# Weight sums stored from another queue, the last product's loads moved up, and a scale on another engine, in an encoder layer in float32

## The chip, the core and the metric

The kernel runs on one core of one Trainium2 chip. The metric is device time in microseconds (us) of one execution; lower is better. The engines are TensorE (PE; its weight loads are shown as PEld), VectorE (DVE), ScalarE (ACT), GpSimd (POOL) and SyncE (SP). SyncE, ScalarE and GpSimd each have a queue from which they issue DMA transfers; a queue's instructions are issued in their order, and one that waits holds up those behind it on its engine.

## The reference

One layer of a hybrid encoder for 512 frames of width 1024, in float32. The part that the change touches is the channel mixing at the end:

```python
u, g = jnp.split(x @ w_ffn_in[layer], 2, axis=-1)
h = jax.nn.gelu(causal_dwconv(u, conv_w[layer], conv_b[layer])) * g
x = layer_norm(DEEPNORM_ALPHA * x + h @ w_ffn_out[layer], ln2_g[layer], ln2_b[layer])
```

`w_ffn_in` is 1024 x 5632, so h is 512 x 2816 and `w_ffn_out` 2816 x 1024. Ahead of it stand an input projection, two attention branches with their gates, an output projection and a first layer norm.

## The kernel before

**Precision.** Each float32 operand is split into a rounded part (`hi`, on ScalarE, L103) and the remainder (`lo`, on VectorE, L105). A product of two operands takes three matmuls: hi x hi (L817), hi x lo (L818) and lo x hi (L819). Weights come in by SyncE's queue: class `Stream` loads them up to three pieces ahead into three `raw` buffers (L85), then splits them into a ring of three pairs of tiles. A load waits until VectorE has split the earlier content of its `raw` buffer.

**The feed-forward loop.** The 2816 inner columns are 22 chunks of 128. For each, `ffn_in` (L727 to L729) makes u and g, `activate` applies convolution and GELU, and two chunks form one of 11 pairs.

**The last matrix product** is done by a scheme in which seven products of sums and differences of blocks replace eight products of blocks: the tokens are halved, the rows of `w_ffn_out` go in the two chunks of a pair, and its 1024 columns are halved. Three of the products run in the loop (`second_half`, into PSUM tiles m3, m4 and m1) with weights that `mix_weights` (L777 to L779) forms from a `raw` and a `rawb` tile. The other four need h of all pairs, which is kept in `eh` and `el`, and follow the loop, each over six units of two pairs (the last has one):

- v, into m5, and y, into m2, with weights loaded from `w_ffn_out`;
- x, added into m1, with a sum of three weight blocks;
- z, added into m3, with another sum of weight blocks.

The sums for x and z are formed in the loop by `keep_sums` (L787 to L793): `s7` for x, and for z at once its parts `sh` (ScalarE) and `sl` (VectorE). They are stored to DRAM tensors `s_sum` by L795, three stores of 256 KB a pair. After the loop x is loaded from there like a weight and split again. z is loaded by a second stream (L75) straight into its place, tiles `d`, of which there are six; for each unit there are two loads, the hi parts and the lo parts. The helper `tc.issue_after(st.load)` puts them in SyncE's queue behind the latest load of the first stream.

**The end.** `unit` does one unit of one of these products, for 256 tokens in two blocks of 128 (m1 to m5 thus have a tile for each block). `into` (L892, L894) adds a finished product to the residual `r`, one tile for each of four token blocks, and takes statistics of it (L896). `finish` normalizes a token block: aggregate (L650), variance plus epsilon (L652), its power of -1/2 on GpSimd (L653), then two VectorE passes (L657, L658) and a store from ScalarE's queue (L904). The second token block of z comes last. It is done in two halves of 256 columns, the first into m3, the second into a tile `m6_end` in a PSUM bank that is used anew. For the last token block `finish` splits the second pass: VectorE does 768 columns (L912), GpSimd the other 256 as a product with 1/sigma (L909) and a sum (L910), and three stores (L914) follow.

**Who sets the order.** The program is written in the order of the code, but a scheduler that simulates the engines puts each engine's instructions in a row; what the code fixes is the order of a queue's loads within a stream and the `issue_after` marks. So z's matmuls for the first token block stand among those of y, where the simulated times put them.

Of the kernel before, what the change touches and what calls it, by code (L numbers as in the profile page):

```python
# [13 lines left out]
AF = mybir.ActivationFunctionType  # L14
ALU = mybir.AluOpType
# [34 lines left out]
def r32(ap):  # L50
    return ap.bitcast(F32)
# [77 lines left out]
def tile_block(ctx: ExitStack, tc: tile.TileContext, xT, xN, w_qi, w_ki, w_t, w_v, w_br, w_o, w_fi, w_fo,  # L129
               bg, cw, rel, onehot, lnp, out):  # L130
    nc = tc.nc
# [24 lines left out]
    def pa(name):  # L156
        return psA.tile([128, 512], F32, tag="A", name=name)

    def pb(name):
        return psB.tile([128, 512], F32, tag="B", name=name)  # L160
# [21 lines left out]
    sums = [nc.dram_tensor(f"s_sum{u}", (3, min(2, NP - 2 * u), 128, 512), F32, kind="Internal").ap() for u in range(NU)]  # L182
# [14 lines left out]
    st = Stream(nc, rawp, ring, order, 3, 3, place, POOL_LO)  # L197
    zt = Stream(nc, rawp, ring, kept, 0, 0, place)
# [443 lines left out]
    def bcast(pool, row):  # L642
        t = pool.tile([128, D], F32, name=f"ln{row}")
        nc.gpsimd.dma_start(t, bass.AP(tensor=lnp.tensor, offset=lnp.offset + row * D, ap=[[0, 128], [1, D]]))
        return t

    def norm_stats(r, parts):

        mv = padded(dp, [128, 2], tag="mv", bufs=2, name="mv")
        nc.vector.bn_aggr(mv, parts)  # L650
        rstd = padded(dp, [128, 1], tag="rstd", bufs=2, name="rstd")
        nc.vector.tensor_scalar(rstd, mv[:, 1:2], EPS, None, op0=ALU.add)  # L652
        nc.gpsimd.tensor_tensor(rstd, rstd, mhalf, op=ALU.pow)  # L653
        return mv, rstd

    def norm_apply(dst, r, mv, rstd, g, b, c):
        nc.vector.scalar_tensor_tensor(dst[:, c], r[:, c], mv[:, 0:1], g[:, c], op0=ALU.subtract, op1=ALU.mult)  # L657
        nc.vector.scalar_tensor_tensor(dst[:, c], dst[:, c], rstd, b[:, c], op0=ALU.mult, op1=ALU.add)  # L658
# [124 lines left out]
    def keep_sums(i):  # L783
        def f(_):

            a, b = (t.rearrange("p (k n) -> p k n", k=2) for t in mixing[i])
            nc.vector.tensor_add(b[:, 0], b[:, 0], a[:, 0])  # L787
            whole_ = tp.tile([128, 512], F32, tag="s7", bufs=1, name=f"s7_{i}")
            nc.vector.tensor_add(whole_, a[:, 1], a[:, 0])
            hi = tp.tile([128, 512], F32R, tag="sh", bufs=1, name=f"sh{i}")  # L790
            lo = tp.tile([128, 512], F32R, tag="sl", bufs=1, name=f"sl{i}")
            nc.scalar.activation(hi, b[:, 0], AF.Copy)
            nc.vector.tensor_sub(lo, b[:, 0], r32(hi))  # L793
            for n, half in enumerate((r32(hi), r32(lo), whole_)):
                nc.gpsimd.dma_start(sums[i // 2][n, i % 2], half)  # L795
            return []
        return f

# [13 lines left out]
    def product(pss, h, w, start, stop, blocks=(0, 1), c=slice(0, 512)):  # L812
        (xh_, xl_), (wh, wl) = h, w
        for t in blocks:
            r = slice(t * 128, t * 128 + 128)
            o = pss[t][:, c]
            nc.tensor.matmul(o, xh_[:, r], wh[:, c], start=start, stop=False, skip_group_check=True)  # L817
            nc.tensor.matmul(o, xh_[:, r], wl[:, c], start=False, stop=False, skip_group_check=True)  # L818
            mm = nc.tensor.matmul(o, xl_[:, r], wh[:, c], start=False, stop=stop, skip_group_check=True)  # L819
        return mm.ins  # L820
# [17 lines left out]
    for f in range(FC):  # L838
        if f == 0:
            ups, gps_ = ps0[0], ps0[1]  # L840
        else:
# [5 lines left out]
            if f % 2 == 0:  # L847
                if f == 2:
                    m3, m1 = [[pb(f"{n}_ps{t}") for t in range(2)] for n in ("m3", "m1")]
# [11 lines left out]
    def unit(pss, row, key, u, w, blocks=(0, 1), c=slice(0, 512), start=True):  # L861
        for n in range(min(2, NP - 2 * u)):
            i = 2 * u + n
            part = [x[:, n * 512:n * 512 + 512] for x in w]
            mm = product(pss, (eh[i][:, row], el[i][:, row]), part, start and i == 0, i == NP - 1, blocks, c)
        return mm
# [22 lines left out]
    def into(j, c, ps, by, first=False, stats=None):  # L889
        r = x1[j][:, c]  # L890
        if first:
            nc.vector.scalar_tensor_tensor(r, r, ALPHA, ps, op0=ALU.mult, op1=ALU.add)  # L892
        else:
            nc.vector.scalar_tensor_tensor(r, ps, by, r, op0=ALU.mult, op1=ALU.add)  # L894
        if stats is not None:
            nc.vector.bn_stats(parts2[j][:, stats], r)  # L896

    def finish(j):
        r = x1[j]
        mv, rstd = norm_stats(r, parts2[j])  # L900
        if j < 3:
            for c in (slice(0, 512), slice(512, 1024)):
                norm_apply(r, r, mv, rstd, g2, b2, c)
                nc.scalar.dma_start(out[j * 128:(j + 1) * 128, c], r[:, c])  # L904
            return
        cs = (slice(0, SHARE // 2), slice(SHARE // 2, SHARE), slice(SHARE, 1024))
        for c in (slice(512, 1024), slice(0, 512)):
            nc.vector.scalar_tensor_tensor(r[:, c], r[:, c], mv[:, 0:1], g2[:, c], op0=ALU.subtract, op1=ALU.mult)
        nc.gpsimd.tensor_scalar(r[:, cs[2]], r[:, cs[2]], rstd, None, op0=ALU.mult)  # L909
        nc.gpsimd.tensor_add(r[:, cs[2]], r[:, cs[2]], b2[:, cs[2]])  # L910
        for c in cs[:2]:
            nc.vector.scalar_tensor_tensor(r[:, c], r[:, c], rstd, b2[:, c], op0=ALU.mult, op1=ALU.add)  # L912
        for c in cs:
            nc.scalar.dma_start(out[j * 128:(j + 1) * 128, c], r[:, c])  # L914
# [12 lines left out]
        unit(m5, 1, "v", u, w)  # L927
    g2, b2 = bcast(wp, 2), bcast(wp, 3)
    held = []
    for u in range(NU):  # L930
        unit(m1, 2, "x", u, st.get(f"x{u}"), start=False)
        if u == 0:
            for t in range(2):
                into(t, second_c, m5[t], 1.0, stats=1)
                into(t, first_c, m5[t], -1.0)
    m2 = [pa(f"m2_ps{t}") for t in range(2)]
    for u in range(NU):
        unit(m2, 0, "y", u, st.get(f"y{u}"))
        with tc.issue_after(st.load):
            held.append(zt.get(f"z{u}"))  # L940
        if u < 2:
            into(u, first_c, m1[u], 1.0, stats=0)
            finish(u)
    for u in range(NU):
        mm = unit(m3, 3, "z", u, held[u], (0,), start=False)
        if u == 0:
            for t in range(2):
                into(2 + t, first_c, m2[t], 1.0, stats=0)
                into(2 + t, second_c, m2[t], -1.0)
            into(3, slice(768, 1024), m3[1][:, 256:512], 1.0)  # L950
    into(2, second_c, m3[0], 1.0, stats=1)
    finish(2)
    lo_c, hi_c = slice(0, 256), slice(256, 512)
    end = [None, pb("m6_end")]
# [4 lines left out]
    with tc.issue_after(mm):  # L959
        for u in range(NU):  # L960
            unit(end, 3, "z", u, held[u], (1,), hi_c, start=True)
    into(3, slice(768, 1024), end[1][:, hi_c], 1.0, stats=2)
    finish(3)
    close(wc)
    close(ec)
# [68 lines left out]
```

## Time and profile before

| | |
|---|---|
| median of 3 runs | 773.91 us (773.15 to 774.04) |
| the profiled execution | 773.86 us |
| its span, first to last instruction | 771.7 us |
| mean granted TensorE clock | 0.995 |
| PE busy | 753.8 us |
| DVE busy | 563.6 us |
| ACT busy | 358.4 us |
| POOL busy | 136.3 us |
| DMA engines, mean | 139 GB/s |

All times inside the program are us from the span's start. A row of the timeline has start, duration, engine, line, operation, output <- inputs by the program's names (without buffer numbers: `m_ps` is any of m1 to m5, `d_z` the z weights), shape and count; in square brackets stands the idle time of the engine ahead of it, and what ended it. SPq and ACTq are the issuing of transfers by SyncE and ScalarE. Matmuls are pipelined: a row's duration is longer than the distance to the next one.

### The profile page before, as it was taken

Reading aid. Unit: us, or ns where it says so; the run is one execution under the profiler, and the core shown is the slowest. Engines: PE = TensorE matmul, PEld = TensorE weight load, DVE = VectorE, ACT = ScalarE, POOL = GpSimd, SP = SyncE. Lnnn points to the kernel's source line nnn. Section 1 sums busy time; section 2 is a strip of 40 time slices with the busy share of each in tenths; the row PEclk is TensorE's granted clock in tenths of the full one; section 3 lists DMA queues with packets and bytes.
Section 4 is the critical chain, followed back from the end, with each engine's and each line's share of the span. In section 5 each row is a group of like instructions: output and inputs, shape, how many; then the busy total and the mean of one; then the engine's idle time right before and its main releaser. Section 6 shows DMA issues by size and latency. Waiting matters only on the chain.

```text
span 771.7 us, 9924 instructions
## 1 busy us (share of the span) xinstructions
PE 753.8 (98%) x3597; PEld 630.3 (82%) x3597; DVE 563.6 (73%) x944; ACT 358.4 (46%) x568; POOL 136.3 (18%) x161
## 2 busy tenths in 40 slices
PE   8999999999999999999999999999999999999995
PEld 7788887788888888888888888888888888888874
DVE  5579999977666475548855778767877787777774
ACT  6445654666564756835311534434443344344410
POOL 2002534527814110000000000000000000000011
PEclk9999999999999999999999999999999999999998
DMA  7742332232323323116801453355335434535591
GB/s 247 233 148 82 109 110 69 69 110 82 110 96 112 107 77 123 61 65 215 319 1 42 164 178 124 136 178 175 123 139 177 169 127 141 178 135 190 193 379 59
DMA packets 36336, 107.08 MB, mean 139 GB/s; under 512 B 4536, under 2 KB 4936, under 8 KB 36288
## 3 DMA queue, kind: packets, MB, share of 16 engines
q1 hardware_dynamic: 29264, 87.08, 32.9%
q0 software_dynamic: 4448, 13.09, 4.9%
q10 hardware_dynamic: 2576, 6.29, 3.0%
q8 instruction: 28, 0.46, 0.2%
q14 instruction: 20, 0.16, 0.1%
HBM read 91.48 MB, written 12.87 MB: 135 GB/s over the span
## 4 chain that ended last, share of the span: by engine, by line
PE 75%; DMA 3%; DVE 2%; issue 0%; ACT 0%; POOL 0%; POOLq 0%; ACTq 0%
PE u_ps L728 5%; PE u_ps L729 5%; PE g_ps L729 5%; PE g_ps L728 5%; PE g_ps L727 5%; PE u_ps L727 5%; PE m_ps L818 4%; PE m_ps L819 4%; PE m_ps L817 4%; DMA d_z<-s_sum 3%; PE av_ps L426 2%; PE ga_ps L276 2%; PE ga_ps L277 2%; PE ga_ps L275 2%; PE o_ps L687 2%; PE o_ps L685 2%
## 5 line engine op out<-in xcount | busy, mean ns | idle before, releaser
L727 PE MATMUL u_ps<-x1h,whi_u 128*128 128x512 f32 (+1 forms) x192 | 71.5, 372 | 0.3 <-ACT x1h L710 0.3
L728 PE MATMUL u_ps<-x1l,whi_u 128*128 128x512 f32 (+1 forms) x192 | 71.4, 372 | 0.1
L729 PE MATMUL u_ps<-x1h,wlo_u 128*128 128x512 f32 (+1 forms) x192 | 71.3, 372 | 0.0
L727 PE MATMUL g_ps<-x1h,whi_g 128*128 128x512 f32 (+1 forms) x184 | 69.9, 380 | 0.0
L729 PE MATMUL g_ps<-x1h,wlo_g 128*128 128x512 f32 (+1 forms) x184 | 69.9, 380 | 0.0
L728 PE MATMUL g_ps<-x1l,whi_g 128*128 128x512 f32 (+1 forms) x184 | 69.9, 380 | 0.0
L727 PEld LDWEIGHTS u_ps<-x1h,whi_u 128*128 128x128 f32 x192 | 36.2, 188 | 6.7 <-ACT x1h L710 0.5
L728 PEld LDWEIGHTS u_ps<-x1l,whi_u 128*128 128x128 f32 x192 | 36.2, 188 | 6.5 <-DVE x1l L711 0.3
L729 PEld LDWEIGHTS u_ps<-x1h,wlo_u 128*128 128x128 f32 x192 | 36.2, 188 | 6.3
L729 PEld LDWEIGHTS g_ps<-x1h,wlo_g 128*128 128x128 f32 x184 | 34.6, 188 | 6.6
L728 PEld LDWEIGHTS g_ps<-x1l,whi_g 128*128 128x128 f32 x184 | 34.6, 188 | 6.5
L727 PEld LDWEIGHTS g_ps<-x1h,whi_g 128*128 128x128 f32 x184 | 34.6, 188 | 6.5
L415 DVE TENSOR_TENSOR ptl<-tr_ps,pth 128x512 fp32r<-128x512 f32 (+1 forms) x48 | 27.4, 594 | 13.6 <-ACT pth L414 13.5
L736 POOL MEMSET u<- 128x2 f32 x22 | 2.3, 108 | 183.9 <-DVE c L741 183.9
L105 DVE TENSOR_TENSOR wlo_u<-raw,whi_u 128x1024 fp32r<-128x1024 f32 x22 | 26.9, 1221 | 9.5 <-ACT whi_u L103 9.5
L103 ACT ACTIVATE whi_g<-raw 128x1024 fp32r<-128x1024 f32 x22 | 23.3, 1060 | 20.5 <-PE m_ps L819 13.7
L103 ACT ACTIVATE whi_pa<-raw 128x1024 fp32r<-128x1024 f32 x11 | 11.7, 1062 | 40.8 <-PE u_ps L728 32.3
L742 ACT ACTIVATE c<-c,cwt 128x512 f32<-128x512 f32 x22 | 15.8, 717 | 30.8 <-DVE c L741 30.8
L105 DVE TENSOR_TENSOR wlo_g<-raw,whi_g 128x1024 fp32r<-128x1024 f32 x22 | 26.8, 1218 | 3.9 <-ACT whi_g L103 3.9
L103 ACT ACTIVATE whi_u<-raw 128x1024 fp32r<-128x1024 f32 x22 | 23.3, 1059 | 13.4 <-PE u_ps L728 8.7
L467 POOL TENSOR_TENSOR beta<-beta,keep 128x1280 f32<-128x1280 f32 x8 | 20.5, 2567 | 48.7 <-DVE keep L466 43.2
L414 ACT ACTIVATE pth<-tr_ps 128x512 fp32r<-128x512 f32 (+1 forms) x48 | 23.5, 520 | 11.3 <-PE tr_ps L410 8.9
(562 smaller groups left out, 2224.1 us busy)
## 6 DMA issues: line engine op xcount, KB each, us to landing
raw<-in_w_fi_dram SPq DMA_DIRECT2D x44, 512.0 KB, 3.3
raw<-in_w_t_dram SPq DMA_DIRECT2D x32, 512.0 KB, 3.3
raw<-in_w_fo_dram SPq DMA_DIRECT2D x21, 512.0 KB, 3.4
rawb_p<-in_w_fo_dram SPq DMA_DIRECT2D x11, 512.0 KB, 4.0
d_z<-s_sum SPq DMA_DIRECT2D x10, 512.0 KB, 9.3
raw<-in_w_v_dram SPq DMA_DIRECT2D x8, 512.0 KB, 3.5
raw<-in_w_br_dram SPq DMA_DIRECT2D x8, 512.0 KB, 3.2
raw<-in_w_o_dram SPq DMA_DIRECT2D x8, 512.0 KB, 4.1
```

The source lines that it names most:

```text
L103: nc.scalar.activation(hi[:, :w], t[:, :w], AF.Copy)
L105: self.low = eng.tensor_sub(lo[:, :w], t[:, :w], r32(hi[:, :w])).ins
L414: nc.scalar.activation(th[:, :width], ps[:, :width], AF.Copy)
L415: lows = nc.vector.tensor_sub(tl[:, :width], ps[:, :width], r32(th[:, :width]))
L467: nc.gpsimd.tensor_mul(beta, beta, keep[:, 1:ATT + 1])
L727: nc.tensor.matmul(ps[:, c], wh[:, kc], x1h[:, k, c], start=(k == 0), stop=False)
L728: nc.tensor.matmul(ps[:, c], wh[:, kc], x1l[:, k, c], start=False, stop=False)
L729: nc.tensor.matmul(ps[:, c], wl[:, kc], x1h[:, k, c], start=False, stop=(k == KC - 1))
L742: nc.scalar.activation(c, c, AF.Gelu_apprx_tanh, bias=cwt[:, f, 3:4])
L817: nc.tensor.matmul(o, xh_[:, r], wh[:, c], start=start, stop=False, skip_group_check=True)
L818: nc.tensor.matmul(o, xh_[:, r], wl[:, c], start=False, stop=False, skip_group_check=True)
L819: mm = nc.tensor.matmul(o, xl_[:, r], wh[:, c], start=False, stop=stop, skip_group_check=True)
```

## The change

Three edits. The stores of the weight sums (L795) are issued by SyncE in place of GpSimd. The product with 1/sigma of 256 columns of the last token block (L909) runs on ScalarE, with the scale as a value for each partition, in place of GpSimd. And z's loads are placed earlier: behind the x units 0, 1, 3 and 5 and the y units 0 and 1, where before there was one behind each y unit. With it a sum of 256 columns of m3's second token block into the residual, which was among the z units, stands ahead of y.

```diff
-                nc.gpsimd.dma_start(sums[i // 2][n, i % 2], half)
+                nc.sync.dma_start(sums[i // 2][n, i % 2], half)
...
-        nc.gpsimd.tensor_scalar(r[:, cs[2]], r[:, cs[2]], rstd, None, op0=ALU.mult)
+        nc.scalar.activation(r[:, cs[2]], r[:, cs[2]], AF.Copy, scale=rstd)
...
+    def keep_z():
+        with tc.issue_after(st.load):
+            held.append(zt.get(f"z{len(held)}"))
+
     for u in range(NU):
         unit(m1, 2, "x", u, st.get(f"x{u}"), start=False)
+        if u in (0, 1, 3, 5):
+            keep_z()
         if u == 0:
...
+    into(3, slice(768, 1024), m3[1][:, 256:512], 1.0)
     m2 = [pa(f"m2_ps{t}") for t in range(2)]
     for u in range(NU):
         unit(m2, 0, "y", u, st.get(f"y{u}"))
-        with tc.issue_after(st.load):
-            held.append(zt.get(f"z{u}"))
+        if u in (0, 1):
+            keep_z()
...
-            into(3, slice(768, 1024), m3[1][:, 256:512], 1.0)
```

SyncE's queue after the loop, before: `s_sum0` to `s_sum5` are the units of the stored sums, `raw` tiles take those for x and the weights of y, `d_z0` to `d_z5` are z's units (x2 marks the two loads).

```order
L85 DMA raw_140_0_6384<-s_sum3 128x2x512
L85 DMA raw_141_0_6408<-s_sum4 128x2x512
L85 DMA raw_142_0_6426<-s_sum5 128x512
L85 DMA raw_143_0_6443<-in_w_fo_dram 128x2x512
L85 DMA raw_144_0_6461<-in_w_fo_dram 128x2x512
L85 DMA raw_145_0_6479<-in_w_fo_dram 128x2x512
L85 DMA raw_146_0_6493<-in_w_fo_dram 128x2x512
L75 DMA d_z0_6511<-s_sum0 128x2x512 x2
L85 DMA raw_147_0_6527<-in_w_fo_dram 128x2x512
L75 DMA d_z1_6545<-s_sum1 128x2x512 x2
L85 DMA raw_148_0_6561<-in_w_fo_dram 128x512
L75 DMA d_z2_6579<-s_sum2 128x2x512 x2
```

And the same queue now, from the load of x3 on:

```order
L85 DMA raw_140_0_6384<-s_sum3 128x2x512
L75 DMA d_z0_6402<-s_sum0 128x2x512 x2
L85 DMA raw_141_0_6411<-s_sum4 128x2x512
L75 DMA d_z1_6429<-s_sum1 128x2x512 x2
L85 DMA raw_142_0_6432<-s_sum5 128x512
L85 DMA raw_143_0_6449<-in_w_fo_dram 128x2x512
L75 DMA d_z2_6467<-s_sum2 128x2x512 x2
L85 DMA raw_144_0_6470<-in_w_fo_dram 128x2x512
L85 DMA raw_145_0_6488<-in_w_fo_dram 128x2x512
L75 DMA d_z3_6500<-s_sum3 128x2x512 x2
L85 DMA raw_146_0_6506<-in_w_fo_dram 128x2x512
L75 DMA d_z4_6524<-s_sum4 128x2x512 x2
```

Before, four of z's six units (z2 to z5) stand behind the last weight load; now z0 to z4 stand in front of the last two. On TensorE z0's products for the first token block follow the first two products of x2, and z1 to z5 are spread up to the y4 unit; the rest of y comes behind them.

VectorE's row from the last split of y (L105) to the sum of `m6_end`, before (`m2_ps0` and `m2_ps1` are y's tiles for the two token blocks, `m3_ps0` and `m3_ps1` z's; `r2` and `r3` are the residual of the third and the fourth token block):

```order
L105 TENSOR_TENSOR wlo_y5_6564<-raw_148_0_6561,whi_y5_6563 128x512
L894 SCALAR_TENSOR_TENSOR r2_3602<-m2_ps0_6491,r2_3602 128x512 x2
L894 SCALAR_TENSOR_TENSOR r3_3603<-m2_ps1_6492,r3_3603 128x512 x2
L896 BN_STATS parts2_2_6307<-r2_3602 128x6
L896 BN_STATS parts2_3_6308<-r3_3603 128x6
L894 SCALAR_TENSOR_TENSOR r3_3603<-m3_ps1_4218,r3_3603 128x256
L894 SCALAR_TENSOR_TENSOR r2_3602<-m3_ps0_4217,r2_3602 128x512
L896 BN_STATS parts2_2_6307<-r2_3602 128x6
L650 BN_AGGR mv_6663<-parts2_2_6307 128x2
L652 TENSOR_SCALAR rstd_6665<-mv_6663 128x1
L657 SCALAR_TENSOR_TENSOR r2_3602<-r2_3602,mv_6663,ln2_6380 128x512 x2
L658 SCALAR_TENSOR_TENSOR r2_3602<-r2_3602,rstd_6665,ln3_6382 128x512 x2
```

And now, from the second pair of sums on:

```order
L894 SCALAR_TENSOR_TENSOR r3_3603<-m2_ps1_6505,r3_3603 128x512 x2
L896 BN_STATS parts2_2_6307<-r2_3602 128x6
L894 SCALAR_TENSOR_TENSOR r2_3602<-m3_ps0_4217,r2_3602 128x512
L896 BN_STATS parts2_3_6308<-r3_3603 128x6
L896 BN_STATS parts2_2_6307<-r2_3602 128x6
L894 SCALAR_TENSOR_TENSOR r3_3603<-m3_ps1_4218,r3_3603 128x256
L650 BN_AGGR mv_6663<-parts2_2_6307 128x2
L896 BN_STATS parts2_3_6308<-r3_3603 128x6
L652 TENSOR_SCALAR rstd_6665<-mv_6663 128x1
L657 SCALAR_TENSOR_TENSOR r2_3602<-r2_3602,mv_6663,ln2_6380 128x512 x2
L658 SCALAR_TENSOR_TENSOR r2_3602<-r2_3602,rstd_6665,ln3_6382 128x512 x2
L894 SCALAR_TENSOR_TENSOR r3_3603<-m6_end_6674,r3_3603 128x256
```

The sum of the first 256 columns of the last block and its statistics, which before stood behind L658, now stand ahead of L652. The split of y5 is still ahead of the first row shown, and its matmuls now follow those of z for the first token block.

In the loop the three stores of a pair stand in SyncE's queue directly ahead of the next pair's load of `rawb` (in the second pair one load stands among them). On ScalarE the store of the last block's 256 columns stands between the two 384-column ones; before it stood behind both. No table load is added there.

## The prediction

> **What bounds the kernel now.** I read the page's busy line first, then the chain of work that ended last in order of time, then the end of the program in the timeline.
>
> ```profile
> PE 753.8 (98%) x3597; PEld 630.3 (82%) x3597; DVE 563.6 (73%) x944; ACT 358.4 (46%) x568; POOL 136.3 (18%) x161
> 600.00:620.00 20.00, 20.00 (x90) 16.58 (x89) 14.61 (x22) 8.04 (x12) 1.81 (x5) 1.00 0.49 171
> ```
>
> The matmul unit is busy for 98% of the span, and in the feed-forward loop (second row: busy time of PE, PEld, DVE, ACT, POOL in one stretch, then clock, DMA share, GB/s) for all of it. A change can win only where TensorE stands still: near the end. There the chain leaves PE for DMA:
>
> ```profile
> 729.96 0.45 PE m_ps L817 x2
> 732.37 7.86 DMA d_z<-s_sum
> 740.24 12.10 DMA d_z<-s_sum
> 752.38 0.50 PE m_ps L818
> 762.73 0.44 DVE r L894
> ```
>
> TensorE's own rows there (start, duration, tile, shape, idle time before):
>
> ```profile
> 714.84 0.39 PE L817 MATMUL m_ps<-d_x,eh 128*128 128x512 f32 x1
> 729.80 0.61 PE L817 MATMUL m_ps<-whi_y,eh 128*128 128x512 f32 x2
> 736.23 0.50 PE L817 MATMUL m_ps<-d_z,eh 128*128 128x512 f32 x1 [0.37 <-DMA d_z<-s_sum]
> 752.38 0.50 PE L818 MATMUL m_ps<-d_z,eh 128*128 128x512 f32 x1 [1.12 <-DMA d_z<-s_sum]
> 754.63 0.28 PE L817 MATMUL m_ps<-d_z,eh 128*128 128x256 f32 x1
> 762.42 0.28 PE L819 MATMUL m_end<-d_z,el 128*128 128x256 f32 x1
> ```
>
> Between the first x product and the first y product lie 66 matmuls: (729.80 - 714.84)/66 = 0.2267 us each, with no wait. To the first half-width product lie 165 of them, 37.40 us; the rows give 754.63 - 714.84 = 39.79. So TensorE loses **2.39 us** to waits for z weights, more than the 0.37 and 1.12 in the brackets, because a matmul that restarts is also slower to get going (0.50 for 0.39). The 66 half-width ones run at (762.42 - 754.63)/65 = 0.120 us.
>
> Why z comes late:
>
> ```profile
> 713.05 0.36 SPq L85 DMA_DIRECT2D raw<-s_sum  x1
> 734.74 7.87 SPq L75 DMA_DIRECT2D d_z<-s_sum  x8
> d_z<-s_sum SPq DMA_DIRECT2D x10, 512.0 KB, 9.3
> 713.00:733.00 20.00, 20.00 (x90) 16.55 (x89) 14.85 (x20) 7.95 (x8) 0.00 (x0) 1.00 0.58 188
> 733.00:752.00 19.00, 17.89 (x78) 14.17 (x76) 14.82 (x26) 2.75 (x3) 1.98 (x2) 1.00 1.04 384
> ```
>
> Eight of the twelve z loads are issued after 734.74 and take 9.3 us each: from 733 to 752 the DMA engines are full (share 1.04, 384 GB/s), while the 20 us before run at 0.58.
>
> **The change part by part.**
>
> *z loads moved up.* They now stand in SyncE's queue behind x3, x4, y0, y2, y3 and y4. What TensorE needs first is z0, which the new order puts behind the two first x2 products:
>
> ```profile
> 717.02 1.06 ACT L103 ACTIVATE whi_x<-raw 128x1024 fp32r<-128x1024 f32 x1 [0.26 <-DMA raw<-s_sum]
> 720.73 0.39 PE L818 MATMUL m_ps<-wlo_x,eh 128*128 128x512 f32 x1
> ```
>
> x3 is issued at 713.05 and taken up at 717.02. z0's two halves follow it; at 384 GB/s 512 KB take 1.37 us, so they land near 718.4 and 719.8. TensorE wants them at 720.73 and 720.96: about 1.1 us to spare, the smallest margin. From there each z unit adds 6 x 0.2267 = 1.36 us of TensorE work ahead of the x and y units behind it, which gives their loads and splits that much more time. Following the queue at 1.37 us per 512 KB from 713 on, z1 lands 1 us ahead of its use, and y0 to y5 and z2 to z5 are ready 2 us or more ahead; the last z is in SBUF by about 742 and used near 747.5. So the 2.39 us go, and TensorE's last product would start at 714.84 + 37.40 + 65 x 0.120 = 760.03 in place of 762.42. Bounds: 2.39 at best, nothing if each unit waits as long as now.
>
> *What is late next: VectorE.* Before, y ended long before z, so the third token block was finished while TensorE still multiplied:
>
> ```profile
> 747.92 0.39 PE L819 MATMUL m_ps<-whi_y,el 128*128 128x512 f32 x1
> 748.35 2.48 DVE L894 SCALAR_TENSOR_TENSOR r<-m_ps,r 128x512 f32<-128x512 f32 x4 [2.80 <-PE m_ps L819]
> 750.75 1.28 DVE L896 BATCH_NORM_STATS2 parts<-r 128x6 f32<-128x512 f32 x2
> 751.95 0.41 DVE L894 SCALAR_TENSOR_TENSOR r<-m_ps,r 128x256 f32<-128x256 f32 x1
> 756.53 0.15 DVE L652 TENSOR_SCALAR rstd<-mv 128x1 f32<-128x1 f32 x1
> 757.92 1.41 DVE L658 SCALAR_TENSOR_TENSOR r<-r,rstd,ln 128x512 f32<-128x512 f32 x2
> 759.25 0.41 DVE L894 SCALAR_TENSOR_TENSOR r<-m_ps,r 128x256 f32<-128x256 f32 x1
> 759.70 0.43 DVE L896 BATCH_NORM_STATS2 parts<-r 128x6 f32<-128x256 f32 x1
> 762.73 0.42 DVE L894 SCALAR_TENSOR_TENSOR r<-m_end,r 128x256 f32<-128x256 f32 x1 [2.61 <-PE m_end L819]
> ```
>
> In the new order z runs among x and y, and y's end moves behind it: ahead of the last product into m2's first block stand 161 full and 4 half matmuls, so it starts at 714.84 + 161 x 0.2267 + 0.48 = 751.82, and VectorE takes it up 0.43 later (748.35 - 747.92), at 752.25. From there it has, in its order: four L894 (750.75 - 748.35 = 2.40), four more full-width operations (half of that pace is 1.20 for two, so 2.40), a half-width L894, an aggregate and a half-width L896 (0.41 and 0.43 with little between: 0.9), and from L652 to the end of block 2 what it was, 759.25 - 756.53 = 2.72. Sum 8.42: VectorE comes to m_end at 760.67. TensorE would let it start at 760.03 + 0.31 (762.73 - 762.42) = 760.34. So VectorE is **0.33 us** late, and m_end's add moves from 762.73 to 760.67: **-2.06**. Bounds: -2.39 if VectorE isn't late; about -1.6 if its 0.9 and its pauses are 0.4 longer.
>
> *The 1/sigma product on ScalarE.*
>
> ```profile
> 764.22 0.92 POOL L653 TENSOR_TENSOR rstd<-rstd,mhalf 128x1 f32<-128x1 f32 x1 [6.47 <-DVE rstd L652]
> 765.25 0.96 POOL L909 TENSOR_SCALAR r<-r,rstd 128x256 f32<-128x256 f32 x1
> 765.51 1.17 DVE L912 SCALAR_TENSOR_TENSOR r<-r,rstd,ln 128x384 f32<-128x384 f32 x2
> 766.18 1.45 ACTq L914 DMA_DIRECT2D out_dram<-r  x3
> 766.29 0.97 POOL L910 TENSOR_TENSOR r<-r,ln 128x256 f32<-128x256 f32 x1
> 697.33 0.40 ACT L757 ACTIVATE gh<-sm 128x256 fp32r<-128x256 f32 x1
> ```
>
> GpSimd's 0.96 becomes ScalarE's 0.40 (an ACTIVATE of that shape), with a hand-over to each side of some 0.15: L910 ends near 766.83, not 767.26. But the order of the stores changes too: the 256-wide one now stands second, ahead of VectorE's second 384-wide one, so the third can issue only about 0.4 after 766.85, at 767.25; before, it issued at 766.18 + 1.45 - 0.34 = 767.29. I cost this edit at **nothing** (bounds -0.4 to +0.2); what hides it is VectorE's 1.17 and the queue of three stores. The Trainium skill speaks against it: "ScalarE: Activation LUTs", Rules for kernel authors, gives multiplications to VectorE and budgets 0.3 us for an ACTIVATE and 0.83 ns an element, an estimate of 0.51 us here; by it the sum would be 0.1 us worse. The trace's 0.40 stands.
>
> *Weight sums stored by SyncE.* It adds 33 issues of some 0.34 us to SyncE and takes 33 of 0.54 from GpSimd, which nobody waits for.
>
> ```profile
> 609.00 0.33 SPq L85 DMA_DIRECT2D rawb_p<-in_w_fo_dram  x1
> 609.27 0.54 POOL L795 DMA_DIRECT2D s_sum<-sl  x1
> 613.37 0.69 DVE L777 TENSOR_TENSOR rawb_p<-rawb_p 128x512 f32<-128x512 f32 x1 [3.26 <-DMA rawb_p<-in_w_fo_dram]
> 618.30 1.06 ACT L103 ACTIVATE whi_g<-raw 128x1024 fp32r<-128x1024 f32 x1 [0.38 <-PE g_ps L728]
> 618.55 0.69 DVE L746 TENSOR_TENSOR hp<-g_ps,c 128x512 f32<-128x512 f32 x1 [1.38 <-PE g_ps L729]
> ```
>
> The load of rawb already waited in this queue for the same operation (L793) that the store of sl waits for, so only the issue comes on top: rawb lands 0.4 to 1.1 us later and L777 with it. What covers it: VectorE idles 1.38 at L746 and ScalarE 0.38 at L103, both until TensorE frees a buffer. Cost **0**; if the cover were gone, 0.4 a pair, 10 pairs, 4 us.
>
> The sum goes against the profiled execution: 773.86 (span 771.7 and 2.2 around it; the median of the runs, 773.91, is the same) - 2.06 = **771.8**.
>
> **The rivals.**
>
> 1. *z lands late again, now among x.* The cover of z0 and z1 is 1 us. For it: the 9.3 us landings where the engines are full. Against: x3's 3.97. A wait of 0.6 to 1.5 leaves -1.5 to -0.6: 772.4 to 773.2, take 772.8. Chance 0.17.
>
> 2. *VectorE's tail is longer.* If it comes to m_end another 0.6 later, the gain is 1.45: 772.4. For it: 8.42 us of work in a window of 8.1. Against: each operation's row is known. Chance 0.08.
>
> 3. *Slower: stores hold back weight loads.* Place: SyncE's queue in the loop, at the three stores and the loads behind. It decides from the point where rawb is later by more than the 1.38 us for which VectorE then idles. sh's and sl's stores stand directly ahead of rawb: two issues (0.68 us) and twice 256 KB (0.68 each at 384 GB/s) are 2.0 us, 0.7 beyond VectorE's 1.38; if TensorE lost that in each of 10 pairs, +7 - 2.1: 778.8. The Trainium skill, "DMA: Bandwidth & Descriptors", Queues, rings and completion order, has the reason: descriptors of one issuing queue are taken in ring order, while different queues take turns, so a store on SyncE's queue stands ahead of the load. By that rule alone rawb is later; whether TensorE is, the idle times above decide, and they speak against it. Chance 0.06.
>
> 4. *More than forecast:* VectorE isn't late, and the third store issues 0.3 earlier: 771.2. Chance 0.07.
>
> **How the numbers follow.** The forecast has 0.62, its own range 771.3 to 772.3. About 0.2%, 1.55 us, is what a measurement of this kernel tells from no change, so faster means under 772.36. Faster: forecast 0.62 and rival 4, 0.07: 0.69. Same: rivals 1 and 2: 0.25. Slower: 0.06. The range of 771.0 to 773.2 takes in rivals 1, 2 and 4 and leaves out 3 and the ends.
>
> **What would show it.** Right: no row of PE waiting for d_z; z loads landing between 718 and 743; the DMA share from 713 to 733 near 0.9; no idle time before m_end's L894 on DVE; the span ending 9.0 us after m_end's add starts, as now (771.7 - 762.73); L909 on ACT near 0.4; PE full in the loop. Wrong: a bracket with DMA d_z on PE, PE idle in the loop beside SyncE's L795, or the time from m_end's add to the end changed by over 0.3.

## The result, and the profile after

The changed kernel takes 769.61 us (median of 5 runs, 769.0 to 769.86), the kernel before, run beside it, 774.04. The ratio is 0.9948, 95% interval 0.9933 to 0.9963; by this ratio it is faster by 4.0 us, 2.9 to 5.2 (4.4 by the medians). The prediction said 771.8, in a range of 771.0 to 773.2. Faster was right; the gain is about twice the forecast, and the time lies below the range.

The profiled execution took 769.0 us, with a span of 767.2. Its busy line, and the stretches whose rows the prediction showed (busy time of PE, PEld, DVE, ACT, POOL, then clock, DMA share, GB/s):

```profile
PE 752.5 (98%) x3597; PEld 629.9 (82%) x3597; DVE 564.0 (74%) x944; ACT 359.2 (47%) x569; POOL 117.5 (15%) x127
```
```profile
600.00:620.00 20.00, 20.00 (x90) 16.57 (x89) 14.79 (x20) 7.94 (x11) 0.20 (x2) 1.00 0.50 170
713.00:733.00 20.00, 20.00 (x90) 16.57 (x89) 13.83 (x19) 8.06 (x8) 0.00 (x0) 1.00 0.97 349
733.00:742.00 9.00, 9.00 (x41) 7.46 (x40) 9.00 (x16) 2.13 (x2) 1.98 (x2) 1.00 1.05 387
742.00:752.00 10.00, 10.00 (x47) 8.36 (x46) 3.13 (x5) 0.64 (x1) 0.00 (x0) 1.00 0.17 62
```

TensorE is full in every one of them, and the transfers that filled 733 to 752 now run from 713 to 742. TensorE's own rows after (first x product, first z product, last product) have no bracket:

```profile
714.14 0.62 PE L817 MATMUL m_ps<-d_x,eh 128*128 128x512 f32 x2
...
720.03 0.39 PE L817 MATMUL m_ps<-d_z,eh 128*128 128x512 f32 x1
...
759.35 0.28 PE L819 MATMUL m_end<-d_z,el 128*128 128x256 f32 x1
```

The last block on VectorE, ScalarE and GpSimd (the same timeline, by engine):

```profile
751.56 2.48 DVE L894 SCALAR_TENSOR_TENSOR r<-m_ps,r 128x512 f32<-128x512 f32 x4 [6.84 <-PE m_ps L819]
...
759.83 0.42 DVE L894 SCALAR_TENSOR_TENSOR r<-m_end,r 128x256 f32<-128x256 f32 x1
...
762.59 1.61 DVE L912 SCALAR_TENSOR_TENSOR r<-r,rstd,ln 128x384 f32<-128x384 f32 x2
```
```profile
762.26 0.51 ACT L909 ACTIVATE r<-r,rstd 128x256 f32<-128x256 f32 x1 [18.27 <-POOL rstd L653]
763.24 1.43 ACTq L914 DMA_DIRECT2D out_dram<-r  x3
```
```profile
762.85 0.94 POOL L910 TENSOR_TENSOR r<-r,ln 128x256 f32<-128x256 f32 x1 [0.62 <-ACT r L909]
```

The prediction left out what comes behind the last store: the program's closing instructions, which all stand at the program's last line (L1030 before, L1037 after). Of the view of that line, the two rows that matter; they give shortest, median and longest duration in ns, then the first and last start. Before:

```profile
L1030 POOLq DRAIN  x3: 46/93/4698, 766.2 to 771.5; - x3
L1030 SPq DRAIN  x3: 7/7/7, 769.5 to 771.2; - x3
```

After:

```profile
L1037 POOLq DRAIN  x3: 46/93/1965, 762.8 to 767.0; - x3
L1037 SPq DRAIN  x3: 7/7/7, 766.4 to 766.7; - x3
```

A DRAIN starts while the last work of its engine still runs, and ends behind it, as GpSimd's does here with L910. SyncE waits for every store to land and reaches its first DRAIN at 769.5 before, at 766.4 after. GpSimd's first DRAIN starts with L910 and lasts 4.698 us before, to 770.9, so **before, SyncE and everybody else waited 1.4 us for GpSimd**; after, it lasts 1.965, to 764.8, and SyncE is last. The difference between the two profiled executions, 773.86 - 769.0 = 4.86, by stretches of these rows and those of the prediction:

| stretch | before | after | change | forecast |
|---|---|---|---|---|
| start to the first x product | 714.84 | 714.14 | -0.70 | 0 |
| to TensorE's last product | 47.58 | 45.21 | -2.37 | -2.39 |
| to the sum of m_end (L894) | 0.31 | 0.48 | +0.17 | +0.33 |
| to SyncE's DRAIN, the last store landed | 6.77 | 6.57 | -0.20 | 0 |
| to the end of the span | 2.2 | 0.8 | **-1.4** | 0 |
| outside the span | 2.16 | 1.80 | -0.36 | 0 |

### The profile page after: what moved, and what is told of

Read it like the earlier page. It is cut to its first block, busy times and chain, and to the rows that moved or that the text cites. A ratio compares the mean times of both kernels' runs of the same rounds, so it can differ in the third digit from the quotient of the medians.

```text
span 767.2 us, 9904 instructions
## 1 busy us (share of the span) xinstructions
PE 752.5 (98%) x3597; PEld 629.9 (82%) x3597; DVE 564.0 (74%) x944; ACT 359.2 (47%) x569; POOL 117.5 (15%) x127
## 4 chain that ended last, share of the span: by engine, by line
PE 77%; DVE 4%; issue 0%; ACT 0%; DVEq 0%; ACTq 0%
PE u_ps L728 5%; PE u_ps L729 5%; PE g_ps L729 5%; PE g_ps L728 5%; PE g_ps L727 5%; PE u_ps L727 5%; PE m_ps L817 4%; PE m_ps L818 4%; PE m_ps L819 4%; PE av_ps L426 2%; PE ga_ps L276 2%; PE ga_ps L277 2%; PE ga_ps L275 2%; PE o_ps L687 2%; PE o_ps L685 2%; PE o_ps L686 2%
## 5 line engine op out<-in xcount | busy, mean ns | idle before, releaser
L105 DVE TENSOR_TENSOR wlo_u<-raw,whi_u 128x1024 fp32r<-128x1024 f32 x22 | 26.9, 1221 | 9.2 <-ACT whi_u L103 9.1
L105 DVE TENSOR_TENSOR wlo_g<-raw,whi_g 128x1024 fp32r<-128x1024 f32 x22 | 26.8, 1218 | 3.9 <-ACT whi_g L103 3.9
```

Of the source, the lines that this page charges most:

```text
L105: self.low = eng.tensor_sub(lo[:, :w], t[:, :w], r32(hi[:, :w])).ins
```

## The experiments

Theory 1: GpSimd's closing DRAIN lasts longer the more DMA transfers GpSimd issued in the program (44 before, 11 after), and the change shortened it by taking 33 away. Theory 2: it was long because GpSimd had both L909 and L910 just ahead of it. The first four kernels take the edits apart; they ran on one chip, beside 32 runs of the kernel before with a median of 773.44. Single runs of one kernel differ by nearly 4 us there (771.64 to 775.38), so the profiles decide more than the medians.

**Stores alone.** The kernel before with

```diff
-                nc.gpsimd.dma_start(sums[i // 2][n, i % 2], half)
+                nc.sync.dma_start(sums[i // 2][n, i % 2], half)
```

> The kernel before with the stores of the weight sums (L795) on SyncE's queue, and nothing else. Theory 1 (the last DRAIN on GpSimd takes some 0.085 us for each DMA transfer that GpSimd issued in the program: 3.7 us behind its last operation for 44 transfers in the kernel before, 1.0 for 11 in the kernel after): the DRAIN ends 1.0 us after L910, at 768.3, ahead of SyncE's last wait at 769.6, so the program ends 1.45 us earlier: 772.6. Theory 2 (the DRAIN was long because GpSimd had the product L909 as well as the sum L910 just ahead of it): the DRAIN stays at 3.7 us and the time at 774.0. Rival 3 of the prediction (stores hold back weight loads): slower than 774.0, with idle time of TensorE in the loop.

Measured: 771.78, ratio 0.9979 (0.9969 to 0.9989). Closing instructions, and the sum of m_end:

```profile
L1030 POOLq DRAIN  x3: 46/98/2004, 764.4 to 768.1; - x3
L1030 SPq DRAIN  x3: 7/7/7, 767.5 to 767.9; - x3
```
```profile
760.90 0.42 DVE L894 SCALAR_TENSOR_TENSOR r<-m_end,r 128x256 f32<-128x256 f32 x1 [2.61 <-PE m_end L819]
```

L909 is still on GpSimd, yet the DRAIN is down to 2.004. From m_end's sum to the end of the span (768.4) it takes 7.5 us, where the kernel before takes 771.7 - 762.73 = 8.97. Theory 2 falls. The stores do not slow the loop: TensorE is busy for 250.0 of the 250 us from 440 to 690, as before.

**z's loads alone.** The kernel before with the third edit, shown in part.

```diff
+        if u in (0, 1, 3, 5):
+            keep_z()
...
-        with tc.issue_after(st.load):
-            held.append(zt.get(f"z{u}"))
+        if u in (0, 1):
+            keep_z()
```

> The kernel before with z's loads (and the sum of 256 columns) moved up, and nothing else. Both theories: TensorE's last product 2.4 us earlier, VectorE's sum of m_end 2.2 us earlier, the rest of the end as before with a DRAIN of 3.7 us behind L910: 771.8, the forecast's own figure. If the early z loads are worth more than TensorE's waits for z: under 771.3.

Measured: 771.56, ratio 0.9984 (0.9973 to 0.9995), so 0.4 to 2.1 us faster. Its profile has no wait for z, 45.2 us from the first x product to the last product as in the kernel after, a DRAIN of 4.701, and 769.9 - 760.86 = 9.0 from m_end's sum to the end:

```profile
760.86 0.42 DVE L894 SCALAR_TENSOR_TENSOR r<-m_end,r 128x256 f32<-128x256 f32 x1
```

This is the kernel whose time the prediction added up, with the end as it was. Its time is near the forecast of 771.8, but the kernel before ran at 773.44 beside it: the gain is 1.2 by the ratio, and the forecast 2.06 lies just inside the interval.

**The scale alone.** The kernel before with

```diff
-        nc.gpsimd.tensor_scalar(r[:, cs[2]], r[:, cs[2]], rstd, None, op0=ALU.mult)
+        nc.scalar.activation(r[:, cs[2]], r[:, cs[2]], AF.Copy, scale=rstd)
```

> The kernel before with L909 on ScalarE, and nothing else. Theory 1: the third store no earlier, but L910 ends 3.96 us after m_end's sum starts (as in the kernel after) in place of 4.53, and the DRAIN of still 3.7 us with it, 0.57 us earlier: 773.5. Theory 2: the DRAIN shrinks to 1.0 us: 772.6. The prediction's cost for this edit was nothing: 774.0.

Measured: 772.8, ratio 0.9999 (0.999 to 1.0007): no difference that a measurement shows. In the profile the DRAIN is 4.663 us long, so, like that of z's loads alone, it does not depend on this edit; the end comes 770.7 - 762.28 = 8.4 us after m_end's sum in place of 8.97, because L910 and the DRAIN behind it start earlier:

```profile
L1030 POOLq DRAIN  x3: 46/98/4663, 765.3 to 770.5; - x3
```

**Everything but the stores.** The kernel after with L795 back on GpSimd, the first diff above the other way round.

> The kernel after with the stores of the weight sums back on GpSimd. Theory 1: the DRAIN is 3.7 us long behind L910 and ends 3.96 + 3.7 = 7.66 us after m_end's sum starts, and the program 0.75 later at 8.4, against 7.37 in the kernel after: 1.0 us slower than it, 770.6. Theory 2: as the kernel after, 769.6, DRAIN 1.0.

Measured: 770.87, ratio 0.9969 (0.9959 to 0.9979). The DRAIN is back at 4.658 us, and the end 767.8 - 759.32 = 8.5 us behind m_end's sum: 1.1 more than in the kernel after.

```profile
L1037 POOLq DRAIN  x3: 46/93/4658, 762.3 to 767.5; - x3
L1037 SPq DRAIN  x3: 7/7/7, 765.9 to 767.2; - x3
```

By their ratios the three edits alone gain 1.6, 1.2 and 0.1 us, 2.9 together where the change gains 4.0. The intervals are wide enough for the difference, so these runs do not tell whether the edits help one another.

The next kernels ask what of the transfers the DRAIN counts: their number, their bytes or their packets.

**66 tiny stores more.** The kernel after with

```diff
-            return []
+            return [nc.gpsimd.dma_start(tick[n:n + 1], whole_[0:1, 0:16]) for n in range(66 if i == NP - 1 else 0)][:0]
```

> The kernel after, and GpSimd also issues 66 one-row stores of 64 bytes to a scratch tensor that nobody reads, before the end begins (GpSimd is idle there). GpSimd then issues 77 transfers in place of 11. Theory 1a (the closing DRAIN grows with the number of GpSimd's transfers, 3.68 us behind L910 for 44 and 0.99 for 11, so 0.0815 each and 0.09 besides): DRAIN of 6.4 us behind L910, the end at 3.96 + 6.4 + 0.8 = 11.1 us after m_end's sum in place of 7.4, the time 3.7 us above the kernel after: 773.3. Theory 1b (it grows with the bytes that GpSimd moved): DRAIN 1.0, the time as the kernel after, 769.6. Theory 1c (with the DMA packets: 4448 before and 1808 after on GpSimd's queue, 1.02 ns each): in between, by how many packets the small stores make.

Measured: 814.4, ratio 1.0528 (1.0504 to 1.0553). The end is what theory 1a asked for, 810.3 - 799.18 = 11.1 us from m_end's sum (expected 11.1):

```profile
L1037 POOLq DRAIN  x3: 46/97/7361, 802.2 to 810.0; - x3
```
```profile
799.18 0.41 DVE L894 SCALAR_TENSOR_TENSOR r<-m_end,r 128x256 f32<-128x256 f32 x1
```

GpSimd's queue on the three pages (packets, MB, share), of before, of after and of this kernel:

```profile
q0 software_dynamic: 4448, 13.09, 4.9%
```
```profile
q0 software_dynamic: 1808, 4.44, 1.6%
```
```profile
q0 software_dynamic: 3920, 4.45, 2.3%
```

With the bytes of the kernel after and fewer packets than before, the DRAIN is longer than in either: it goes by the number of transfers. The time as a whole was missed by 41 us, and that is the experiment's own doing. SyncE issues no load between 729.47 and 758.33, and TensorE waits for z's weights:

```profile
764.26 0.80 PE L817 MATMUL m_ps<-d_z,eh 128*128 128x512 f32 x1 [18.82 <-DMA d_z<-s_sum]
```

The small stores read the last s7 and waited for one another's landing (41.1 us in 16 waits). The load of z1, issued at 758.33, waited for the landing of a small store: SyncE's waits for them before z's loads are 28.3 us, the longest 26.2. That z's tile lies where s7 lay would account for it, but this was not tried.

**One of three stores on GpSimd.** The kernel after with

```diff
-                nc.sync.dma_start(sums[i // 2][n, i % 2], half)
+                (nc.gpsimd if n == 2 else nc.sync).dma_start(sums[i // 2][n, i % 2], half)
```

> The kernel after with one of the three stores a pair (s7) on GpSimd: 22 transfers of GpSimd. Theory 1a: DRAIN of 0.09 + 22 x 0.0815 = 1.9 us behind L910; it ends 3.96 + 1.9 = 5.9 us after m_end's sum starts, ahead of SyncE's last wait at 6.6, so the time is that of the kernel after, 769.6.

Measured: 770.34, ratio 0.9957 (0.9944 to 0.9969), as the kernel after within the interval.

```profile
L1037 POOLq DRAIN  x3: 46/98/2867, 763.7 to 768.1; - x3
L1037 SPq DRAIN  x3: 7/7/7, 767.5 to 767.8; - x3
```

**No transfer on GpSimd.** The kernel after with `nc.gpsimd.dma_start` replaced by `nc.sync.dma_start` throughout.

> The kernel after with every DMA issue of GpSimd moved to SyncE (the 11 that are left are the small inputs and the window table at the start and four rows of layer-norm values). Theory 1a: DRAIN of 0.1 us behind L910; no gain from it, since SyncE's wait for the last store already ends last by 1.6 us; from m_end's sum to the end 7.4 as in the kernel after. The start may be some us longer, since SyncE's queue then waits for the window table with weight loads behind it: 769.6 to 775.

Measured: 771.07, ratio 0.9967 (0.9954 to 0.9979). The DRAIN hardly outlasts L910's 0.94, and the end is no earlier for it, 770.0 - 762.55 = 7.45 after m_end's sum; the profiled start (first x product at 716.81) was longer, as feared.

```profile
L1037 POOLq DRAIN  x3: 40/82/1051, 765.5 to 769.7; - x3
```

Eleven profiles together, the last kernel of this section left out (the DRAIN starts with L910, so L910's own duration is taken off):

| kernel | GpSimd's transfers | DRAIN less L910, us | m_end's sum to the end of the span, us |
|---|---|---|---|
| none on GpSimd | 0 | 0.11 | 7.45 |
| after; after again | 11 | 1.03; 1.02 | 7.37; 7.34 |
| stores alone; scale back | 11 | 1.03; 1.03 | 7.50; 7.48 |
| one of three | 22 | 1.93 | 7.58 |
| before; z alone | 44 | 3.73; 3.72 | 8.97; 9.04 |
| scale alone; all but stores | 44 | 3.72; 3.72 | 8.42; 8.48 |
| 66 tiny more | 77 | 6.42 | 11.12 |

The third column is 0.11 + 0.082 for each transfer, to 0.02 us. GpSimd's other instructions do not count: the kernel with no transfer still has 116 of them (POOL on its page; the kernel after has 127 with its 11 transfers), and its DRAIN is 0.11 behind L910.

**The scale back on GpSimd**, in the kernel after (the third diff the other way round), and **the kernel after once more** beside it:

> The kernel after with L909 back on GpSimd. Theory 1 (with 11 transfers of GpSimd the DRAIN is 1.0 us behind L910, wherever L909 runs): L910 ends 4.5 us after m_end's sum starts in place of 3.96, the DRAIN at 5.5, ahead of SyncE's last wait at 6.6; the third store issues 4.56 after it in place of 4.43. 0.1 us above the kernel after: 769.7. Theory 2 (the last operation on GpSimd makes the DRAIN long): DRAIN 3.7, 1.5 us above it.

> The kernel after, unchanged, beside the one above: 769.6. TensorE from the first x product to the last product 45.2 us in each profile (no wait for z), and the start, up to the last product of the first projection, anywhere between 23.2 and 24.4 us, as in the nine profiles so far; if the 0.8 us by which the kernel after started earlier belonged to the change, this profile would show 23.5 again.

Measured: 769.51 (ratio 0.9954, 0.9937 to 0.9972) and 769.11 (0.995, 0.9932 to 0.9969). With the stores off GpSimd the scale's place is worth 0.1 us in the profiles, 7.48 against 7.37 and 7.34, and nothing in the medians. The last product of the first projection (L241), by which the start is judged, in the profile of before, then of the stores alone, then of the kernel after once more:

```profile
24.31 0.34 PE L241 MATMUL qi_ps<-xh,wlo_qi 128*128 128x384 f32 x1
```
```profile
23.32 0.34 PE L241 MATMUL qi_ps<-xh,wlo_qi 128*128 128x384 f32 x1
```
```profile
23.93 0.34 PE L241 MATMUL qi_ps<-xh,wlo_qi 128*128 128x384 f32 x1
```

The second kernel starts as the first one does by its program, and is 1.0 us earlier; the third stands in between. What sets this start, and with it the 0.70 us in the table above, stays open. With up to 11 transfers on GpSimd the row stands at 22.91 to 23.93 in six profiles, with 22 or more at 24.31 to 24.52 in five; but everything but the stores, with 44, has 23.00, so that number alone does not decide it.

**A shorter end.** The kernel after with

```diff
-SHARE = 768
+SHARE = 896
...
-            nc.scalar.dma_start(out[j * 128:(j + 1) * 128, c], r[:, c])
+            (nc.sync if c is cs[2] else nc.scalar).dma_start(out[j * 128:(j + 1) * 128, c], r[:, c])
```

> The kernel after with the last block's share on ScalarE and GpSimd cut from 256 to 128 columns (VectorE's two operations are 448 wide in place of 384) and its store issued by SyncE. In the kernel after VectorE's second L912 takes 1.08 us beside GpSimd's L910 where the first takes 0.62, and the third store issues 4.43 us after m_end's sum starts. If L910 at half its width ends before the second L912 would start, that operation takes 0.66 and the last store issues about 4.1 after m_end's sum: 0.3 us faster than the kernel after, 769.3, hardly more than runs differ. If the second L912 is slow for another reason, it stays near 1.1: 769.6 or a little more.

Measured: 769.64, ratio 0.9955 (0.9941 to 0.9968): no better than the kernel after. L910 at half its width still takes 0.85 (0.94 before), the second L912 beside it 0.875 (the first 0.685), and VectorE's two operations together 1.48:

```profile
762.65 1.48 DVE L912 SCALAR_TENSOR_TENSOR r<-r,rstd,ln 128x448 f32<-128x448 f32 x2
```

The end comes 767.1 - 759.89 = 7.2 us after m_end's sum, 0.15 earlier; a measurement does not show that.

## Why the prediction was right or wrong

**z's loads: right, in mechanism and size.** TensorE loses no time to z, and 47.58 - 45.21 = 2.37 us go, against 2.39. z0's halves were to land at 718.4 and 719.8, for products from 720.73 on, all of it 0.70 later than in the profile after. The view of z's tiles there, loads and landings:

```profile
L75 SPq DMA_DIRECT2D d_z<-s_sum x12: 404/460/614, 712.7 to 735.4; - x12
...
DMA to landing us min/median/max: 5.0/6.3/8.8
```

The first load, issued at 712.7, lands at 717.7 at the earliest, and the first z product runs at 720.03 without a wait. The DMA share from 713 to 733 is 0.97 (I said near 0.9), and by 742 the transfers are nearly over (0.17 from there to 752). What I had not seen is that the 2.39 was itself one draw. TensorE in the profile of the stores alone, where z's loads stand as before:

```profile
713.89 0.62 PE L817 MATMUL m_ps<-d_x,eh 128*128 128x512 f32 x2
...
750.45 0.50 PE L818 MATMUL m_ps<-d_z,eh 128*128 128x512 f32 x1 [0.81 <-DMA d_z<-s_sum]
...
760.58 0.28 PE L819 MATMUL m_end<-d_z,el 128*128 128x256 f32 x1
```

The stretch takes 46.69 us here, and 46.94 in the profile of the scale alone; without waits for z it is 45.2 or 45.3 in every profile. So the edit saves TensorE 1.5 to 2.4 us, and 2.37 agrees so well with 2.39 because both start from the same profile of before.

**VectorE late at the end: right, a little too large.** y's sums start at 751.56, 37.42 after the first x product; forecast were 752.25 - 714.84 = 37.41. VectorE then needs 8.27 us to m_end's sum, not 8.42, and is 0.17 late, not 0.33. The mis-sized term is the 0.9 for the half-width sum, the aggregate and the half-width statistics, which took 0.78 (756.35 to 757.13). There is no idle time ahead of m_end's L894, as forecast.

**The scale on ScalarE: nothing, as forecast, though not as costed.** The ACTIVATE took 0.51, not the 0.40 of the row that I chose. That row has a constant for its scale, this one a value for each partition. The Trainium skill, "ScalarE: Activation LUTs", What ACT_TABLE_LOAD costs, gives 186 ns and 0.833 an element with constants, and 93 more for each operand of that kind: estimates of 0.40 and 0.49, and the trace agrees with both. In a kernel with 44 transfers of GpSimd the edit would shorten the end by 0.55 (8.42 to 8.48 in place of 8.97 to 9.04), because L910, and the DRAIN with it, starts 0.5 earlier behind m_end's sum; I had not seen this. Nor is the nothing reached as I reckoned. I had VectorE's L912 at 1.17 and the third store held up by the queue. In the kernel after the two L912 take 1.61 beside L910 and end at 764.20, and the third store, issued at 764.25, carries what the second of them wrote: 4.42 behind m_end's sum, where before it was 4.56. An earlier L910 and a later L912 nearly cancel.

**Stores on SyncE: the step that failed.** "It adds 33 issues of some 0.34 us to SyncE and takes 33 of 0.54 from GpSimd, which nobody waits for" and "Cost **0**". The first half held: TensorE is full in the loop, and the load of rawb takes no longer to land (page, median us to landing 3.7; 4.0 before), so rival 3 fell. Nine waits for it sum to 26.4 us, before to 25.9. Of the pair that the prediction quoted, SyncE's load, then the wait, 3.04 for 3.26, with the same cover behind it:

```profile
608.65 0.44 SPq L85 DMA_DIRECT2D rawb_p<-in_w_fo_dram  x1
...
612.43 0.69 DVE L777 TENSOR_TENSOR rawb_p<-rawb_p 128x512 f32<-128x512 f32 x1 [3.04 <-DMA rawb_p<-in_w_fo_dram]
...
617.85 0.69 DVE L746 TENSOR_TENSOR hp<-g_ps,c 128x512 f32<-128x512 f32 x1 [1.40 <-PE g_ps L729]
```

The Trainium skill's rule of ring order ("DMA: Bandwidth & Descriptors", Queues, rings and completion order), on which that rival stood, has no price that this trace shows: from the issue of the load to L777 it is 3.78 us behind the stores, and 4.37 before (609.00 to 613.37). The second half was wrong: at the very end everybody waits for GpSimd. 33 x 0.082 = 2.7 us of its DRAIN go, of which 1.4 had been on the path. The chain of before ended in this DRAIN, and I read past it:

```profile
766.25 1.01 POOLq L1030
```

The row shows 1.01 us, a slice of the instruction; the view of line 1030 shows all 4.698. My check "the span ending 9.0 us after m_end's add starts, as now" took this stretch for a constant without asking what fills it, and it is there that the trace after says no: 7.37.

**The rest of the gap.** With these 1.4 us the sum would have been 770.4, and the profiled execution took 769.0. The table gives 0.70 of the other 1.4 to the start, 0.20 to the landing of the stores and 0.14 to z and VectorE; 0.36 us lie outside the span. This part is nearly constant for one built kernel, and differs between kernels. In the mean it is 2.13 to 2.21 in the three without z's edit (before, stores alone, scale alone) and 1.77 to 1.84 in five with it (z alone, all but stores, after, scale back, a shorter end). But three more with z's edit, with 22, 77 and no transfers of GpSimd, have 2.14, 2.16 and 2.34. So z's edit may be worth these 0.36 too, yet does not decide them by itself, and what fills this part stays open; the prediction took it as unchanged. Rival 4, 771.2 with 0.07, was nearest in size, but of its mechanism, an earlier third store, only 0.14 us came (0.20 at its landing), and VectorE was late.

## What to carry to other kernels

Follow the chain of waits to the very last instruction, and view the closing line by engine: it costs time like any other, and here one engine's closing work was 1.4 us of a 4 us gain. An engine that nobody waits for during the program may be waited for at its end, so count the transfers that GpSimd issues; when its closing DRAIN ends ahead of the last landing, fewer of them bring nothing (0, 11 and 22 ended alike). And read a stall's size from several executions before it becomes a term: the waits for z were 1.5 us in one and 2.4 in another.

## What the runs showed of the hardware

GpSimd's closing DRAIN took 0.11 us and 0.082 for each DMA transfer that GpSimd had issued, from 0 to 77 transfers, whatever their size, and long after they were issued (the last store of the kernel before at 685.4, 81 us ahead of the DRAIN). At L910's place in the kernel after, the end of L910 leaves 766.4 - 763.79 = 2.6 us until SyncE is done, so some 30 transfers are free there.

VectorE's second L912 took 1.077 us in the kernel after and 0.606 with the scale back on GpSimd. Rows of the view of L912, after and then scale back:

```profile
L912 DVE SCALAR_TENSOR_TENSOR r<-r,rstd,ln x2: 617/847/1077, 762.6 to 763.1; 128x384 f32<-128x384 f32 x2
```
```profile
L912 DVE SCALAR_TENSOR_TENSOR r<-r,rstd,ln x2: 606/626/646, 762.6 to 763.2; 128x384 f32<-128x384 f32 x2
```

In the kernel after it starts at 763.1, behind the start of L910 (762.85), and ends 0.4 behind L910's end; with the scale back it starts ahead of L910. The Trainium skill, "SBUF — State Buffer", SBUF: two separate sides, has VectorE and GpSimd share a pair of ports; of a VectorE operation with two inputs in SBUF and a GpSimd operation that reads SBUF, the one that starts first holds it for its whole instruction. The trace agrees for L910, which reads two tensors. It does not for L909 on GpSimd, a product with one tensor: with the scale back it runs from 762.33 to 763.29, and the first L912 starts at 762.59 and is not held up (0.646). No run here shows why the two differ.
